# Gate and up projections with half of the depth as Strassen block products, weight sums made by accumulating transfers, and the feed-forward in two parts

## The chip, the cores and the metric

The kernel runs on one core of a Trainium2 chip. Its engines work in parallel, each through its own queue of instructions in order: TensorE (PE) multiplies, with its weight loads (PEld) beside it; VectorE (DVE) and ScalarE (ACT) work elementwise; GpSimd (POOL) does small work and issues transfers; SyncE (SP) issues transfers. The metric is the device time of one execution in microseconds (us), the median of several runs.

## The reference

One layer of a streaming encoder: 256 tokens, 2048 channels, float32. Three mixers with gates, an attention over a memory of 256 tokens, and a feed-forward. The change concerns the last of these alone:

```
def _swiglu(h, w_gu, w_down):
    g, u = jnp.split(h @ w_gu, 2, axis=-1)
    return (jax.nn.silu(g) * u) @ w_down

x = x + _swiglu(_rms(x, norm_ffn[i]), w_gu[i], w_down[i])
```

h is [256, 2048], w_gu [2048, 11264] (gate and up, 5632 columns each), w_down [5632, 2048].

## The kernel before

All large products keep float32 accuracy with the tensor engine's float32r kind: each operand is the sum of a high part, rounded to float32r, and a low part, and a product is three matmuls (high x high, high x low, low x high). The activations are split once into tiles such as `x2T_h` and `x2T_l`, [128 channels, 16 k-tiles, 256 tokens]. The weights are split as they come.

`gemm_i` is the product that carries most of the work: two tiles of 128 tokens by 512 columns of weights, accumulated over `nk` k-tiles of 128 channels in two banks of PSUM (`acc`). The weights come by `load_w` in blocks of four k-tiles, 1 MB each, into `raw` (two buffers), issued on SyncE. `split_w` makes `whi` (a cast on ScalarE, L116) and `wlo` (the difference on VectorE, L117) out of two k-tiles at a time, with four buffers each. Twelve matmuls use such a pair (L146 to L148: two token tiles, two k-tiles, three matmuls). A buffer of `whi` is free when these are done. At the end `evac` reads the two banks.

The stage of gate and up is a loop over 11 chunks of 512 columns. For each chunk there is one `gemm_i` for gate (evacuated by ScalarE with SiLU into `gt`, L1006), one for up (evacuated by VectorE, multiplied into `gt`, L1010), and `to_operand`, in which TensorE transposes the chunk (L812) and ScalarE and VectorE split it into `hT_h` and `hT_l` (L206, L207), which hold all 44 k-tiles. So the stage has 22 products. Then four `gemm_i` over 44 k-tiles multiply by w_down, and VectorE adds `x1`, the residual, into the output. `x2T_h` and `x2T_l` are made by `to_operand` after each quarter of the product with w_xo (L844: `x1` out of PSUM).

The order on each queue is fixed when the program is built, by a scheduler that follows the order of the code and two priorities: `WPRI` for the loads and splits of weights, `EPRI` for evacuations. A queue's instruction waits for semaphores of other queues or of transfers, and everything behind it waits with it.

## Time and profile before

| what | value |
|---|---|
| median of 3 runs | 2051.26 us (2050.34 to 2051.73) |
| the profiled execution, span from first to last instruction | 2048.7 us |
| stage of gate and up in it | 1294.40 to 1796.97 us, 22 products |
| w_down in it | 1796.97 to about 2044 us |
| HBM read, mean over the span | 374.06 MB, 184 GB/s with the writes |
| granted TensorE clock | 1.000 |

The span leaves out what lies before the first and after the last instruction. "Busy" is the time in which an engine has at least one instruction under way. A row of a group gives the line, the engine, the operation, the tile written and the tiles read, the shape, the count after an x, then busy time in us, the mean of one in ns, and the idle time of the engine ahead of them with what ended it. Rows of matmuls overlap, so their mean is not their cost. A row of transfers gives the tile, the queue, the count, the size and the median us from issue to landing. A row with two times joined by a colon is a stretch of the span: its length, then the busy time of PE, PEld, DVE, ACT and POOL with the number of instructions, the granted clock, the share of the transfer engines and GB/s. A row that begins with a time alone is one of the timeline: start, duration, engine, instruction.

### The profile page before, as it was taken

What the parts mean: (1) busy time and instruction counts of PE and PEld (TensorE: products, weight loads), DVE (VectorE), ACT (ScalarE), POOL (GpSimd) and SP (SyncE); (2) the same over time, 40 slices, a digit from 0 to 9 for tenths busy, and PEclk for the clock granted to TensorE, in tenths of its full rate; (3) what the DMA queues carried; (4) which work ended last, traced back from release to release, by engine and by line L of the source; (5) the groups of instructions that cost most, each with busy time, mean ns of one, the idle gap of its engine ahead of it and who ended that gap; (6) DMA issues with size and microseconds to landing.
All of it is one profiled execution on the core that took longest, in us unless ns stands there. A gap on an engine that the chain in (4) does not pass through costs nothing.

```text
span 2048.7 us, 25114 instructions
## 1 busy us (share of the span) xinstructions
PE 2039.7 (100%) x9880; PEld 1670.9 (82%) x9880; DVE 1251.7 (61%) x1804; ACT 966.0 (47%) x1308; POOL 73.7 (4%) x142
## 2 busy tenths in 40 slices
PE   9999999999999999999999999999999999999999
PEld 7998888777777788888888888888888888888887
DVE  7967885769887857645544655445444444444443
ACT  8555556544344445554544545444444444433332
POOL 1001202000000000011000100000000000000000
PEclk9999999999999999999999999999999999999999
DMA  8555455445555555765555444555555555555553
GB/s 309 186 174 165 152 179 186 155 172 174 180 183 188 192 171 195 271 218 175 175 185 185 144 145 164 185 185 185 185 185 185 185 185 185 185 185 195 195 197 132
DMA packets 60406, 377.78 MB, mean 184 GB/s; under 512 B 6912, under 2 KB 8064, under 8 KB 18816
## 3 DMA queue, kind: packets, MB, share of 16 engines
q1 hardware_dynamic: 56880, 367.42, 51.4%
q0 software_dynamic: 2112, 6.82, 1.2%
q10 hardware_dynamic: 1296, 1.95, 0.3%
q8 instruction: 77, 1.26, 0.2%
q14 instruction: 41, 0.34, 0.1%
HBM read 374.06 MB, written 2.10 MB: 184 GB/s over the span
## 4 chain that ended last, share of the span: by engine, by line
PE 99%; DVE 0%; DMA 0%; issue 0%; SPq 0%; ACT 0%; DVEq 0%; ACTq 0%
PE acc L146 29%; PE acc L148 29%; PE acc L147 28%; PE acc L169 2%; PE acc L170 2%; PE acc L171 2%; PE sm L422 1%; PE sm L812 1%; PE sm L952 1%; PE sm L978 1%; PE sm L449 1%; PE sm L215 0%; PE sm L896 0%; DMA raw<-in_w_in_dram 0%; DVE xT_l L210 0%
## 5 line engine op out<-in xcount | busy, mean ns | idle before, releaser
L117 DVE TENSOR_TENSOR wlo<-raw,whi 128x1024 fp32r<-128x1024 f32 (+2 forms) x700 | 834.7, 1194 | 697.7 <-ACT whi L116 694.3
L116 ACT CAST whi<-raw 128x1024 fp32r<-128x1024 f32 (+2 forms) x700 | 715.9, 1025 | 941.3 <-PE acc L148 816.9
L146 PE MATMUL acc<-whi,x2T_h 128*128 128x512 f32 x704 | 281.2, 399 | 0.0
L148 PE MATMUL acc<-whi,x2T_l 128*128 128x512 f32 x704 | 277.9, 395 | 0.0
L147 PE MATMUL acc<-wlo,x2T_h 128*128 128x512 f32 x704 | 277.2, 394 | 0.0
L147 PE MATMUL acc<-wlo,xT_h 128*128 128x512 f32 (+2 forms) x704 | 264.6, 377 | 1.8 <-DVE wlo L117 1.6
L148 PE MATMUL acc<-whi,xT_l 128*128 128x512 f32 (+2 forms) x704 | 265.3, 378 | 0.0
L146 PE MATMUL acc<-whi,xT_h 128*128 128x512 f32 (+2 forms) x704 | 262.4, 377 | 0.2
L148 PEld LDWEIGHTS acc<-whi,x2T_l 128*128 128x128 f32 x704 | 132.2, 188 | 33.4
L147 PEld LDWEIGHTS acc<-wlo,x2T_h 128*128 128x128 f32 x704 | 132.2, 188 | 31.4
L146 PEld LDWEIGHTS acc<-whi,x2T_h 128*128 128x128 f32 x704 | 132.2, 188 | 30.1
L147 PEld LDWEIGHTS acc<-wlo,xT_h 128*128 128x128 f32 x704 | 132.0, 188 | 29.8 <-DVE wlo L117 3.3
L146 PEld LDWEIGHTS acc<-whi,xT_h 128*128 128x128 f32 x704 | 131.5, 188 | 29.6 <-issue 3.2
L148 PEld LDWEIGHTS acc<-whi,xT_l 128*128 128x128 f32 x704 | 132.1, 188 | 27.8 <-issue 1.9
L146 PE MATMUL acc<-whi,hT_h 128*128 128x512 f32 x352 | 139.1, 395 | 0.0
L147 PE MATMUL acc<-wlo,hT_h 128*128 128x512 f32 x352 | 139.1, 395 | 0.0
L148 PE MATMUL acc<-whi,hT_l 128*128 128x512 f32 x352 | 139.0, 395 | 0.0
L148 PE MATMUL acc<-whi,eT_l 128*128 128x512 f32 x256 | 101.6, 397 | 0.0
L147 PE MATMUL acc<-wlo,eT_h 128*128 128x512 f32 x256 | 101.4, 396 | 0.0
L146 PE MATMUL acc<-whi,eT_h 128*128 128x512 f32 x256 | 101.2, 395 | 0.0
L169 PE MATMUL acc<-xT_h,whi 128*128 128x256 f32 x352 | 99.9, 284 | 0.0
L170 PE MATMUL acc<-xT_l,whi 128*128 128x256 f32 x352 | 99.5, 283 | 0.0
(375 smaller groups left out, 2837.0 us busy)
## 6 DMA issues: line engine op xcount, KB each, us to landing
raw<-in_w_gu_dram SPq DMA_DIRECT2D x88, 1024.0 KB, 4.8
raw<-in_w_in_dram SPq DMA_DIRECT2D x68, 1024.0 KB, 4.8
raw<-in_w_down_dram SPq DMA_DIRECT2D x44, 1024.0 KB, 4.7
raw<-in_w_xkv_dram SPq DMA_DIRECT2D x32, 1024.0 KB, 4.7
raw<-in_w_ii_dram SPq DMA_DIRECT2D x22, 1024.0 KB, 5.0
raw<-in_w_out_dram SPq DMA_DIRECT2D x16, 1024.0 KB, 5.0
raw<-in_w_xq_dram SPq DMA_DIRECT2D x16, 1024.0 KB, 4.8
raw<-in_w_xo_dram SPq DMA_DIRECT2D x16, 1024.0 KB, 4.8
```

The lines of the kernel that those rows point to most:

```text
L116: S.copy(hi[:, :n], raw[:, c0:c1])
L117: V.tensor_tensor(lo[:, :n], raw[:, c0:c1], hi[:, :n].bitcast(F32), ALU.subtract)
L146: PE.matmul(o, sh, h, start=(kt == 0), stop=False)
L147: PE.matmul(o, sh, lw, start=False, stop=False)
L148: PE.matmul(o, xl[:, kt, t * P:(t + 1) * P], h, start=False, stop=(kt == nk - 1))
L169: PE.matmul(po, h, xh[:, kt, :], start=(kt == 0), stop=False)
L170: PE.matmul(po, h, xl[:, kt, :], start=False, stop=False)
L171: PE.matmul(po, lo[:, j * P:(j + 1) * P], xh[:, kt, :], start=False, stop=(kt == nk - 1))
L422: PE.matmul(pb[:, i * T:(i + 1) * T], bT[q:q + 32, i, c, :], u[q:q + 32, c, :], start=True, stop=True, tile_position=(q, 0))
L449: PE.matmul(py[q:q + 32, :], cT[:, i, 4 * c + j, :], xs[j][:, i * T:(i + 1) * T], start=(i == 0), stop=(i == 1), tile_position=(0, q))
L812: PE.transpose(px[:, j * T + t * P:j * T + (t + 1) * P], srcs[t][:, (kp + j) * P:(kp + j + 1) * P], ident)
L952: PE.matmul(pS[:, t * T:(t + 1) * T], qx[:, qi, d, t * P:(t + 1) * P], kx[:, ki, d], start=(d + i == 0), stop=(d == 3 and i == 2))
```

## The change

The stage's product becomes `gemm_s`. Its first eight k-tiles are as before. The other eight are four pairs of k-tiles, and for each pair and the two token tiles the operand is seen as two by two blocks of 128x128, the weights as two by two blocks of 128x256 (`b11`, `b12`, `b21`, `b22`, each over four pairs, 1024 columns in all). Seven block products instead of eight give the result (Strassen's scheme in Winograd's form): four of them with sums of blocks of weights. The sums are made in place, in SBUF, by transfers that add (`wsum`, on GpSimd's queue): b11 += b12, b12 += b22, b22 += b11, b21 += b22, in this order. The weights of these eight k-tiles come into `sraw`, 2 MB with one buffer. The seven products go where their results are wanted in PSUM, or into a bank `sm` of their own; VectorE adds and subtracts them there (L238). The sums of the operand's blocks are made once, into `x2S_h` and `x2S_l`, by `pairs_operand`.

The feed-forward runs in two parts: chunks 0 to 5 of gate and up, then w_down over their 24 k-tiles, added into `x1`; then chunks 6 to 10, and w_down over their 20 k-tiles.

In the core of the diff line numbers are left out; the changed file's comments were removed, so its lines are numbered otherwise (the cast and the difference of `split_w` are L122 and L123 there, those of `parts` L202 and L203).

```diff
-KF = FF // P
+FF_PARTS = ((0, 6), (6, 11))
...
+    def wsum(dst, src):
+        with tc.high_priority(offset=WPRI):
+            nc.gpsimd.dma_start(dst, src, accum_op=ALU.add)
...
+    NS = 8
+    A11, A12, A21, A22, S1, S3, S2, S4 = range(8)
+    def gemm_s(xh, xl, sop, nk, src, off, evac, seven=True):
+        pp = [acc(), acc()]
+        n, no = 512, nk - NS
+        for k in range(0, no, 4):
...
+        raw = spool[0].tile([P, NS * n], F32, tag="sraw", name=nm("sraw"))
+        for i in range(2):
+            load_w(src[off:off + P * 4 * n].rearrange("(p f) -> p f", p=P), 4 * n,
+                   raw[:, i * 4 * n:(i + 1) * 4 * n])
+            off += P * 4 * n
+        rv = raw.rearrange("p (i q h c) -> p q h i c", q=2, h=2, c=256)
+        b11, b12, b21, b22 = (rv[:, q, h] for q in range(2) for h in range(2))
+        def parts(b):
+            hi = wp.tile([P, 1024], F32R, tag="whi", name=nm("whi"), bufs=4)
+            lo = wp.tile([P, 1024], F32R, tag="wlo", name=nm("wlo"), bufs=4)
...
+                S.copy(hi, b)
+                V.tensor_tensor(lo, b, hi.bitcast(F32), ALU.subtract)
+            return hi, lo
+        def product(o, i, b, start, stop):
+            hi, lo = b
+            for p in range(4):
+                sh, sl = sop(0, p, i), sop(1, p, i)
+                PE.matmul(o, sh, hi[:, p], start=start and p == 0, stop=False)
+                PE.matmul(o, sh, lo[:, p], start=False, stop=False)
+                PE.matmul(o, sl, hi[:, p], start=False, stop=stop and p == 3)
+        def kept(o):
+            u = spool[0].tile([P, 256], F32, tag="u", name=nm("u"), bufs=4)
+            with tc.high_priority(offset=EPRI):
+                S.copy(u, o)
+            return u
...
+        w21, w22, w11 = parts(b21), parts(b22), None
...
+        product(c(0, 0), A12, w21, False, False)
+        product(c(0, 1), S4, w22, False, True)
+        u1 = kept(side(A11, parts(b11)))
+        v(c(0, 0), c(0, 0), u1, ALU.add)
+        wsum(b11, b12)
+        wsum(b12, b22)
+        wsum(b22, b11)
+        u5 = kept(side(S1, parts(b11)))
+        p6 = side(S2, parts(b22))
+        wsum(b21, b22)
+        v(u1, p6, u1, ALU.add)
+        v(c(0, 1), c(0, 1), u5, ALU.add)
+        v(c(0, 1), c(0, 1), u1, ALU.subtract)
+        evac(0, pp[0])
+        product(c(1, 0), A22, parts(b21), False, True)
+        p7 = side(S3, parts(b12))
+        v(c(1, 1), c(1, 1), u5, ALU.add)
+        v(u1, p7, u1, ALU.add)
+        v(c(1, 0), c(1, 0), u1, ALU.add)
+        v(c(1, 1), c(1, 1), u1, ALU.subtract)
+        evac(1, pp[1])
+        return off
...
-        to_operand([x1[:, t, n * 512:(n + 1) * 512] for t in range(2)], gTh, gTl, 4 * n,
-                   "norm_ffn")
+        srcs = [x1[:, t, n * 512:(n + 1) * 512] for t in range(2)]
+        if n < 2:
+            to_operand(srcs, gT[0], gT[1], 4 * n, "norm_ffn")
+        else:
+            pairs_operand(srcs, n - 2, "norm_ffn")
...
-    for n in range(FF // 512):
...
-        off = gemm_i(gTh, gTl, KD, a["w_gu"], off, 512, evg)
-        off = gemm_i(gTh, gTl, KD, a["w_gu"], off, 512, evu)
-        to_operand(sg, hTh, hTl, 4 * n)
...
+    for c0, c1 in FF_PARTS:
+        nk = 4 * (c1 - c0)
+        hTh = p3.tile([P, nk, T], F32R, tag="hh", name=nm("hT_h"))
+        hTl = p3.tile([P, nk, T], F32R, tag="hl", name=nm("hT_l"))
+        for n in range(c0, c1):
...
+            gu_off = gemm_s(gT[0], gT[1], sop, KD, a["w_gu"], gu_off, evg)
+            gu_off = gemm_s(gT[0], gT[1], sop, KD, a["w_gu"], gu_off, evu)
+            to_operand(sg, hTh, hTl, 4 * (n - c0))
+        for n in range(4):
+            def ev(t, po, n=n, last=(c1 == FF // 512)):
...
+                    if not last:
+                        d = x1[:, t, n * 512:(n + 1) * 512]
+                        V.tensor_tensor(d, po, d, ALU.add)
+                        return
...
+            gemm_i(hTh, hTl, nk, a["w_down"], (n * FF + c0 * 512) * 512, 512, ev)
```

Three queues show where the change stands in the program. The names in the rows are the tiles with a running number; what stands in brackets are the queues whose semaphores the instruction waits for (DMASW are GpSimd's transfers, DMAHW SyncE's).

ScalarE before, in one product of the stage: the eight casts, each waiting for its load and for TensorE's use of the buffer.

```order
L116 CAST whi_12138<-raw_12136 128x1024 [waits DMAHW6_49,DVE_49,PE_49]
L116 CAST whi_12154<-raw_12136 128x1024 [waits DVE_49,PE_49]
L116 CAST whi_12172<-raw_12170 128x1024 [waits DMAHW7_49,DVE_49,PE_49]
L116 CAST whi_12188<-raw_12170 128x1024 [waits DVE_49,PE_49]
L116 CAST whi_12206<-raw_12204 128x1024 [waits DMAHW0_49,DVE_49,PE_49]
```

ScalarE after, from the first cast out of `sraw` to the first casts of the next product: the blocks 21, 22 and 11, then block 11 with its sum, two copies, blocks 22, 21 and 12 with their sums, and then the next product's n0 and n1.

```order
L202 CAST whi_12411<-sraw_12408 128x1024 [waits DMAHW4_49,DMAHW5_49,PE_49,Activation_49]
L202 CAST whi_12415<-sraw_12408 128x1024 [waits PE_49,Activation_49]
L202 CAST whi_12443<-sraw_12408 128x1024 [waits PE_49,Activation_49]
L202 CAST whi_12466<-sraw_12408 128x1024 [waits DMASW0_49,PE_49,Activation_49]
L217 COPY u_12460<-sm_12447 128x256 [waits PE_49]
L217 COPY u_12483<-sm_12470 128x256 [waits PE_49]
L202 CAST whi_12485<-sraw_12408 128x1024 [waits DMASW2_49,DVE_49]
L202 CAST whi_12507<-sraw_12408 128x1024 [waits DMASW3_49,DVE_49]
L202 CAST whi_12523<-sraw_12408 128x1024 [waits DMASW1_49,DVE_49]
L122 CAST whi_12565<-raw_12563 128x1024 [waits DMAHW6_49,DVE_49]
L122 CAST whi_12581<-raw_12563 128x1024 [waits DVE_49,PE_49]
```

Behind the plain casts now stand four that wait for GpSimd's transfers, and the next product's casts stand behind these.

GpSimd after, the transfers of one product (before it had none in this stage, its last rows being the reciprocal roots of the norm) and the first of the next:

```order
L115 DMA sraw_12201<-sraw_12201 128x4x256 [waits DMAHW0_49,DMAHW1_49,DMASW3_49,DVE_49]
L115 DMA sraw_12201<-sraw_12201 128x4x256 [waits DMASW4_49]
L115 DMA sraw_12201<-sraw_12201 128x4x256 [waits DMASW5_49]
L115 DMA sraw_12201<-sraw_12201 128x4x256 [waits DMASW6_49]
L115 DMA sraw_12408<-sraw_12408 128x4x256 [waits DMAHW4_49,DMAHW5_49,DMASW7_49,DVE_49]
```

The second, third and fourth wait for the transfer ahead of each.

TensorE after, at the end of one product and the start of the next: the last two block products (`acc_12132` from block 21, `sm_12320` from block 12) and the next product's first matmuls.

```order
L210 MATMUL acc_12132<-whi_12300,x2T_h 128x256 [waits Activation_49]
L210 MATMUL sm_12320<-whi_12316,x2T_h 128x256 [waits PE_49,Activation_49]
L211 MATMUL acc_12132<-wlo_12301,x2T_h 128x256 [waits DVE_49]
...
L185 MATMUL acc_12338<-whi_12342,x2T_h 128x512 [waits Activation_49]
L185 MATMUL acc_12339<-whi_12342,x2T_h 128x512
L211 MATMUL sm_12320<-wlo_12317,x2T_h 128x256 [waits DVE_49]
```

Two matmuls of the next product were moved ahead of the rest of the last block product, but none ahead of the product with block 21.

SyncE after: the load of `sraw` for the next product, between the loads of `raw` for that product and for the one after it.

```order
L101 DMA raw_12770<-in_w_gu_dram 128x2048 [waits DMAHW6_49,DVE_49]
L101 DMA raw_12804<-in_w_gu_dram 128x2048 [waits DMAHW7_49,DVE_49]
L101 DMA sraw_12838<-in_w_gu_dram 128x2048 [waits DMASW7_49,DMASW6_49,DMAHW0_49,DMASW5_49,DMAHW1_49,DMASW4_49,DVE_49]
L101 DMA sraw_12838<-in_w_gu_dram 128x2048
L101 DMA raw_12993<-in_w_gu_dram 128x2048 [waits DMAHW2_49,DVE_49]
```

The reload waits for all four of GpSimd's transfers of the product before, and for VectorE's last read; before, a load waited for a buffer of `raw` alone.

More of the change, by code (lines that the diff above doesn't have):

```diff
@@ L154, in gemm_i, with c, side, v @@
             evac(t, pp[t])
+        return off
[5 more added lines that the diff above has]
+        for k in range(0, no, 4):
+            raw = load_w(src[off:off + P * 4 * n].rearrange("(p f) -> p f", p=P), 4 * n)
+            off += P * 4 * n
+            for k2 in range(0, 4, 2):
+                hi, lo = split_w(raw, k2 * n, (k2 + 2) * n)
+                for t in range(2):
+                    for j in range(2):
+                        kt = k + k2 + j
+                        h, lw = hi[:, j * n:(j + 1) * n], lo[:, j * n:(j + 1) * n]
+                        sh = xh[:, kt, t * P:(t + 1) * P]
+                        PE.matmul(pp[t], sh, h, start=(kt == 0), stop=False)
+                        PE.matmul(pp[t], sh, lw, start=False, stop=False)
+                        PE.matmul(pp[t], xl[:, kt, t * P:(t + 1) * P], h, start=False, stop=False)
+        raw = spool[0].tile([P, NS * n], F32, tag="sraw", name=nm("sraw"))
+        for i in range(2):
+            load_w(src[off:off + P * 4 * n].rearrange("(p f) -> p f", p=P), 4 * n,
+                   raw[:, i * 4 * n:(i + 1) * 4 * n])
+            off += P * 4 * n
+        rv = raw.rearrange("p (i q h c) -> p q h i c", q=2, h=2, c=256)
[3 more added lines that the diff above has]
+            lo = wp.tile([P, 1024], F32R, tag="wlo", name=nm("wlo"), bufs=4)
+            hi, lo = (x.rearrange("p (i c) -> p i c", c=256) for x in (hi, lo))
+            with tc.high_priority(offset=WPRI):
+                S.copy(hi, b)
[13 more added lines that the diff above has]
+            return u
+        def c(t, h):
+            return pp[t][:, h * 256:(h + 1) * 256]
+        w21, w22, w11 = parts(b21), parts(b22), None
+        if not seven:
+            w11, w12 = parts(b11), parts(b12)
+            for t in range(2):
+                for h, q, w in ((0, 0, w11), (1, 0, w12), (0, 1, w21), (1, 1, w22)):
+                    product(c(t, h), 2 * t + q, w, False, q == 1 and h == 1)
+            for t in range(2):
+                evac(t, pp[t])
+            return off
+        def side(i, w):
+            o = sm()[:, :256]
+            product(o, i, w, True, True)
+            return o
+        def v(dst, x, y, op):
+            with tc.high_priority(offset=EPRI):
+                V.tensor_tensor(dst, x, y, op)
+        product(c(0, 0), A12, w21, False, False)
[19 more added lines that the diff above has]
+        evac(1, pp[1])
@@ L989, in tile_block @@
                      resid_evac(n, 2, lambda t: x1[:, t, n * 512:(n + 1) * 512]))
[L990 to L991 removed]
+        srcs = [x1[:, t, n * 512:(n + 1) * 512] for t in range(2)]
+        if n < 2:
+            to_operand(srcs, gT[0], gT[1], 4 * n, "norm_ffn")
+        else:
+            pairs_operand(srcs, n - 2, "norm_ffn")
     finish_rstd(2, 6)
[L993 removed]
     poolA.release()
     p3 = tc.alloc_tile_pool(name="p3", bufs=1)
[L998 removed]
@@ L999, in tile_block @@
-    hTl = p3.tile([P, KF, T], F32R, name="hT_l")
-    off = 0
-    for n in range(FF // 512):
-        sg = [t2k("gt", 2), t2k("gt", 2)]
-        def evg(t, po, sg=sg):
-            with tc.high_priority(offset=EPRI):
-                S.activation(sg[t], po, AF.Silu, scale=rst[:, 6 + t:7 + t])
-        def evu(t, po, sg=sg):
-            with tc.high_priority(offset=EPRI):
-                V.scalar_tensor_tensor(sg[t], po, rst[:, 6 + t:7 + t], sg[t], ALU.mult, ALU.mult)
-        off = gemm_i(gTh, gTl, KD, a["w_gu"], off, 512, evg)
-        off = gemm_i(gTh, gTl, KD, a["w_gu"], off, 512, evu)
-        to_operand(sg, hTh, hTl, 4 * n)
@@ L1014, in tile_block @@
-    off = 0
-    for n in range(4):
-        def ev(t, po, n=n):
-            o = t2k()
-            with tc.high_priority(offset=EPRI):
-                for c in range(0, 512, 256 if n == 3 else 512):
-                    d = slice(c, c + (256 if n == 3 else 512))
-                    g = slice(n * 512 + d.start, n * 512 + d.stop)
-                    V.tensor_tensor(o[:, d], po[:, d], x1[:, t, g], ALU.add)
-                    (nc.sync if c else nc.scalar).dma_start(out[t * P:(t + 1) * P, g], o[:, d])
-        off = gemm_i(hTh, hTl, KF, a["w_down"], off, 512, ev)
+    spool[0] = p3
```

51 lines of the change are left out of this document (47 added, 4 removed).

## The prediction

> **What bounds the kernel now.** I read the page first, its busy shares and its chain, then the stage of gate and up alone, then single rows for the prices.
>
> ```profile
> span 2048.7 us, 25114 instructions
> PE 2039.7 (100%) x9880; PEld 1670.9 (82%) x9880; DVE 1251.7 (61%) x1804; ACT 966.0 (47%) x1308; POOL 73.7 (4%) x142
> PE 99%; DVE 0%; DMA 0%; issue 0%; SPq 0%; ACT 0%; DVEq 0%; ACTq 0%
> 1294.40:1796.97 502.57, 502.57 (x2202) 405.31 (x2200) 244.67 (x225) 212.34 (x227) 1.47 (x4) 1.00 0.52 184
> L146 PE MATMUL acc<-whi,x2T_h 128*128 128x512 f32 x704 | 281.2, 399 | 0.0
> L117 DVE TENSOR_TENSOR wlo<-raw,whi 128x1024 fp32r<-128x1024 f32 x176 | 215.6, 1225 | 244.7 <-ACT whi L116 243.3
> L116 ACT CAST whi<-raw 128x1024 fp32r<-128x1024 f32 x176 | 184.6, 1049 | 266.1 <-PE acc L148 262.4 <-DMA raw<-in_w_gu_dram 3.7
> ```
>
> TensorE carries the chain: 99% of it, and in the stage of gate and up (fourth row: from the first product with x2T to the first with hT) it is busy for all 502.57 us, VectorE for half, ScalarE for less, the transfers for 0.52. One of the 22 products there costs 502.57 / 22 = 22.84 us. The splits stand idle waiting for TensorE (last row), so nothing but TensorE's own work sets the end. Work taken from TensorE is gain, as long as nothing that feeds it becomes later than it.
>
> The 394 to 399 ns of a row is not what a matmul costs: rows overlap. The spacing of the starts is.
>
> ```profile
> 2037.26 0.39 PE L146 MATMUL acc<-whi,hT_h 128*128 128x512 f32 x1
> ...
> 2044.02 0.39 PE L148 MATMUL acc<-whi,hT_l 128*128 128x512 f32 x1
> ```
>
> These are the first and the last of 30 rows in a run: 6.76 / 29 = 0.233 us for 512 columns. For 256 columns the first and the last of nine rows:
>
> ```profile
> 99.99 0.28 PE L169 MATMUL acc<-xT_h,whi 128*128 128x256 f32 x1
> ...
> 100.94 0.28 PE L171 MATMUL acc<-xT_h,wlo 128*128 128x256 f32 x1
> ```
>
> 0.95 / 8 = 0.119 us: half the columns, half the time, nothing lost to the smaller tile.
>
> **TensorE's own work.** Before, a product is 96 matmuls of 512 columns: 96 x 0.233 = 22.4 us. After, it is 48 of these (11.2 us) and seven block products of 12 matmuls with 256 columns (84 x 0.119 = 10.0 us): 21.2 us. The gain is 1.2 us a product, 22 x 1.2 = 27 us in all, if TensorE never waits.
>
> **What the four accumulating transfers put in its way.** They are one chain: the second reads what the first writes, the third the second's and so on, each waits for the landing of the one ahead. The first waits for VectorE to have split block 11, and that split needs a buffer of whi, of which there are four: it waits until TensorE is done with the third pair of k-tiles (n2 of n0 to n3). At its end, the fourth block (w21 with sums) is cast only when the last transfer has landed; on ScalarE the casts of the next product stand behind that one, and on SyncE the next 2 MB of sraw, since sraw has one buffer. TensorE's queue has nothing of the next product to do meanwhile. So per product there is a ring: landing of the fourth transfer (T) -> cast and split -> last two block products -> n0, n1, n2 of the next product -> split of block 11 -> four transfers -> T. Worked from T:
>
> ```profile
> L210 DVE SCALAR_TENSOR_TENSOR x2T_l<-sm,pp,x2T_h 128x256 fp32r<-128x256 f32 x4 | 1.7, 477 | 1.1 <-ACT x2T_h L209 1.1
> 1339.82 0.40 PE L148 MATMUL acc<-whi,x2T_l 128*128 128x512 f32 x1
> 1340.25 1.05 ACT L116 CAST whi<-raw 128x1024 fp32r<-128x1024 f32 x1 [1.75 <-PE acc L148]
> 1.48 4.31 PE L229 MATMUL acc<-ev 128*128 128x256 f32 x12 [1.48 <-DVE ev L226]
> 4.76 1.03 PE L229 MATMUL acc<-ev 128*128 128x256 f32 x4
> ```
>
> - Cast of w21 1.05, its low part 1.22: T + 2.3. Then a sum of 128x256 out of PSUM (0.48 by the first row, the nearest of that shape) and the low part of w12, 1.22: T + 4.0.
> - The product with w21, 12 matmuls of 256 columns. TensorE comes out of a wait here. At the kernel's start, after a wait, 12 equal rows (fourth row) begin at 1.48; the last four begin at 4.76 (fifth row). So the first eight take 3.28 / 8 = 0.41 us each, while the last four fit in 1.03: TensorE runs at about half its speed for some 3 us after it has stood, though the page's granted clock reads full there. I take double price: from T + 2.3, 11 more x 0.24 = T + 4.9.
> - The product with w12, 12 x 0.119 = 1.4: T + 6.3. n0, n1 and n2, 36 matmuls x 0.233 = 8.4: T + 14.7. Their casts and splits (three at 1.05 and 1.22) lie beside, ahead of TensorE.
> - A cast starts 0.43 us after the start of the last matmul that it waits for (second and third row), 0.2 after the end by spacing: 0.2 + 1.05 + 1.22 = 2.5. The first transfer can be issued at T + 17.2; some 0.3 for the hops between queues: T + 17.5.
>
> Beside it the reload of sraw: it may be issued when w12 is split, T + 4.0, and brings 2 MB.
>
> ```profile
> raw<-in_w_gu_dram SPq DMA_DIRECT2D x88, 1024.0 KB, 4.8
> GB/s 300 430 96 0 116 355 403 0 0 27 205 430 212 0 96 321 423 48 0 157 423 294 0 102 171 423 178 0 96 348 430 0 0 177 410 287 0 109 177 437
> ```
>
> One megabyte lands in 4.8 us, a second one behind it at the peak rate of the second row (430 GB/s, 1.2 us a column) 2.4 us later: T + 11.2; the three blocks out of it are cast and split by 1.05 + 3 x 1.22: T + 15.9. That is inside 17.5, by 1.6 us; between both loads in 4.8 and one after the other in 9.6 us it is T + 13.5 to T + 18.3, so it may cost up to 0.8 us a product. I take 17.5.
>
> So a product takes 17.5 + 4L, L being one accumulating transfer from issue to landing. L is in no row of this trace: nothing accumulates, nothing goes from SBUF to SBUF. The nearest rows are GpSimd's own loads and SyncE's by size:
>
> ```profile
> L868 POOL DMA_DIRECT2D gt<-in_x_dram x8: 536/536/538, 667.8 to 877.2; - x8
> DMA to landing us min/median/max: 3.3/4.1/5.0
> ...
> L661 POOL DMA_DIRECT2D t2k<-in_bias_dram x8: 536/566/626, 233.1 to 408.7; - x8
> DMA to landing us min/median/max: 2.7/4.8/5.7
> raw<-in_w_qk_dram SPq DMA_DIRECT2D x4, 512.0 KB, 3.2
> gt<-in_x_dram POOLq DMA_DIRECT2D x8, 256.0 KB, 4.1
> t2k<-in_bias_dram POOLq DMA_DIRECT2D x8, 192.0 KB, 4.8
> out_dram<-t2k ACTq DMA_DIRECT2D x2, 128.0 KB, 1.9
> ```
>
> GpSimd's 256 KB take 3.3 at best, 4.1 in the middle. SyncE's 512 KB take 3.2 and its 1024 KB 4.8, so 512 KB more cost 1.6. An accumulation of 512 KB reads 512 KB and what is there, another 512 KB: 768 KB more than the 256 KB row, 1.5 x 1.6 = 2.4. In the ring no load is under way while the four run, so I start from the best case: 3.3 + 2.4 = 5.7 us. Counted by bytes written alone it would be 3.3 + 0.8 = 4.1, and the whole 2051 + 22 x (17.5 + 16.4 - 22.84) = 2295; I count what is read, because the sum cannot be formed without both operands. The low end is 2.7, GpSimd's fastest landing of any size. The high end: the pieces are runs of 1 KB (512 of them against 128), so issuing may grow from 0.54 to 2.1 us, and on the slowest 256 KB row that is 5.0 + 2.4 + 1.6 = 9.0. The ends of the sum are then 28.3 and 53.5 us a product.
>
> The Trainium skill (Collectives: The Full Stack, the part on why ReduceScatter is half of AllGather) says that an adding transfer runs at half the rate because it emits two reads for each piece, not because the adding costs. By that rule L is the 5.7 above, by the rate of a plain copy 4.1, and the time 2435 or 2295. No row of this trace shows which.
>
> **The sum.** 17.5 + 4 x 5.7 = 40.3 us a product against 22.84: 17.5 us more, x 22 = 385 us. The gain of 27 us is in it, since TensorE's work is no longer the path.
>
> Edits that cost nothing. The feed-forward in two parts: eight additions of 128x512 into x1 (the second row below has this shape, 0.69 us) beside w_down's products; the second part's first write of hT waits for the end of the first part's w_down, but comes only two products later, over 42 us. The end of part one is a second change from up to w_down, but its first products read k-tiles finished long before. The operand's sums for the block products (16 additions of 128x128 with their splits) are wanted only after n3 of the first product, 11.2 us after TensorE begins there; if they come late it is once, a few us.
>
> ```profile
> L1010 DVE SCALAR_TENSOR_TENSOR gt<-acc,rst,gt 128x512 f32<-128x512 f32 x21 | 14.8, 744 | 0.0
> L207 DVE TENSOR_TENSOR hT_l<-sm,hT_h 128x512 fp32r<-128x512 f32 x20 | 12.9, 686 | 12.0 <-ACT hT_h L206 12.0
> ```
>
> VectorE's load per product is 11 splits x 1.22 + 7 sums x 0.48 + half of two evacuations at 0.74 + half of two low parts of hT at 0.69: 13.4 + 3.4 + 0.7 + 0.7 = 18.2 us, below 40.3 and also below 21.2. Of the seven sums only the one counted is in the ring.
>
> The sum is made on the profiled execution, 2048.7 us of span; the median of the runs is 2051.26, so 2.6 us lie outside it and stay. 2051.3 + 385 = 2436, taken as **2435 us**.
>
> **The rivals.**
>
> *Short transfers.* L may be near a small fixed price. At 2.7 to 3.3 us the sum gives 5.5 to 7.9 us more a product, 120 to 173 us: 2171 to 2224 us. For it: hardware-issued 512 KB land in 3.2. Against: GpSimd's never did below 3.3 at half the bytes. The Trainium skill (DMA: Bandwidth & Descriptors, Anatomy of one DMA) gives a GpSimd transfer 2.0 us + bytes / 436 GB/s, 3.2 us for 512 KB as a copy; by that estimate the time is 2215. The trace's 256 KB rows, 2.6 by the formula and 3.3 to 5.0 here, do not agree. Chance 10%, with everything below 2240.
>
> *Long transfers.* If GpSimd's descriptors for 1 KB pieces or the addition itself are slow, L is above 8 and the time above 2051 + 22 x (49.5 - 22.84) = 2637, up to 2725 at L = 9. For it: GpSimd's 192 KB in 1.5 KB rows already take 4.8 in the middle, longer than its 256 KB. Against: those ran beside weight loads. Chance 8%.
>
> *Hidden transfers, the other side.* If the four land ahead of TensorE's need, the path is TensorE's work again, and the time is 2051 - 27 = 2024. The place is the block product with w21: it must not wait. That needs 17.5 + 4L at most 22.84 to be even, L of 1.3 us; for the full gain about 1 us. For it: they are issued ahead, GpSimd has nothing else to do in this stage (4 rows, 1.47 us). Against: the fastest of all groups of transfers in the trace, 128 KB to the output, has a median of 1.9 us. Chance 2%; another 1% for landing within 0.2% of before.
>
> *Weights instead of sums.* The reload of sraw at its upper end (9.6 us) adds 0.8 x 22 = 18 us: 2453. It is inside the range.
>
> **How the numbers follow.** About 79% for the exposed chain at L of 3.5 to 8, 10% shorter, 8% longer, 3% not slower at all. The likeliest is the first, at 5.7: 2435. The range is its two ends, 17.5 + 14 = 31.5 us a product, 2051 + 190 = 2241, and 2637: 2240 to 2640; the ends of L beyond it hold the 18% left out. Within 0.2% (4 us, about what a measurement of this kernel can tell from no change) is 1%, faster 2%, slower 97%.
>
> **What would show it.** In the changed kernel's profile: TensorE no longer at 100% but at 21.6 / 40.3, near 55%, in the stage of gate and up, full elsewhere; a row of 88 transfers sraw<-sraw of 512 KB with a median near 5.7 us (this alone decides between the cases); ScalarE's casts of sraw waiting for these, with the third and fourth the longest; the stage some 887 us long. Matmuls with 256 columns at spacings of 0.119 where TensorE runs, 0.24 just after a wait. It would be wrong if TensorE's queue held work of the next product in those waits, or if the four transfers overlapped one another.

## The result, and the profile after

The changed kernel takes 2454.3 us (median of 4 runs, 2453.6 to 2454.7) against 2051.5 us before (2050.3 to 2052.9): 1.196 times the time, 95% interval 1.195 to 1.198. The prediction was 2435 us, 2240 to 2640. The profiled execution's span is 2452.7 us.

The page of the changed kernel, the rows that answer to those shown of before: the span, the busy shares, the granted clock in 40 slices, and the chain that ended last.

```profile
span 2452.7 us, 27437 instructions
PE 2140.2 (87%) x10672; PEld 1782.1 (73%) x10672; DVE 1397.5 (57%) x2066; ACT 1046.9 (43%) x1422; POOL 184.9 (8%) x230
PEclk9999999999999999999998777777799887777799
PE 73%; DMA 20%; issue 3%; ACT 2%; DVE 2%; POOL 0%; SPq 0%; ACTq 0%; DVEq 0%; POOLq 0%
```

TensorE carried 99% of the chain before; now it is 73%, and transfers that were nowhere on it hold 20%. TensorE's busy time has even grown (2039.7 to 2140.2 us) though it has less to do: the third row shows the clock at 0.7 to 0.8 in the slices of gate and up, full in w_down (the 9s between them and at the end).

The same stage, as two stretches (12 products of part one, 10 of part two: from the first product with x2T to the first with hT; columns as before):

```profile
1295.12:1787.80 492.68, 326.31 (x1623) 278.75 (x1622) 206.47 (x256) 160.42 (x188) 62.52 (x52) 0.76 0.60 153
1925.03:2335.50 410.47, 272.93 (x1350) 233.50 (x1349) 169.16 (x205) 129.05 (x148) 50.81 (x40) 0.75 0.59 147
```

Together 903.15 us where 502.57 us stood: 41.05 us a product instead of 22.84. That is 400.6 of the 402.8 us lost; w_down, the operand's sums and the second part cost next to nothing. TensorE is busy in 66% of it, at a granted clock of 0.75.

What waits, from the view of waits (engine and line, what it waited for, us in all, times, the longest), and then the view of the tile `sraw` on GpSimd, the transfers that are waited for (ns of an issue, first and last start, and us from issue to landing):

```profile
ACT whi L202 <- DMA sraw<-sraw: 379.9, 66, 7.5
POOL sraw L115 <- DMA sraw<-sraw: 296.5, 66, 5.1
PE sm L210 <- ACT whi L202: 226.9, 66, 9.0
```

```profile
L115 POOL DMA_DIRECT2D sraw<-sraw x88: 1255/1272/1389, 1308.7 to 2323.2; - x88
DMA to landing us min/median/max: 5.4/5.4/6.0
```

88 adding transfers, 5.4 us each, with hardly any spread. The first row is 66 waits, three a product: ScalarE's casts of the first, third and fourth sum (by the time block 12 is cast, its sum has landed). The second is GpSimd waiting for the transfer ahead of each, and the third TensorE behind ScalarE.

One whole turn of the ring, from GpSimd's rows of the timeline (start, duration of the issue, what GpSimd waited for) and the same turn in the chain that ended last (start, us, what):

```profile
1514.43 1.27 POOL L115 DMA_DIRECT2D sraw<-sraw  x1 [22.26 <-DVE wlo L203]
1520.14 1.26 POOL L115 DMA_DIRECT2D sraw<-sraw  x1 [4.44 <-DMA sraw<-sraw]
1525.83 1.27 POOL L115 DMA_DIRECT2D sraw<-sraw  x1 [4.42 <-DMA sraw<-sraw]
1532.06 1.26 POOL L115 DMA_DIRECT2D sraw<-sraw  x1 [4.96 <-DMA sraw<-sraw]
1555.64 1.27 POOL L115 DMA_DIRECT2D sraw<-sraw  x1 [22.31 <-DVE wlo L203]
```

```profile
1532.06 5.43 DMA sraw<-sraw
...
1537.57 1.05 ACT whi L202
1538.62 0.02 issue
1538.64 0.93 DVE wlo L203
...
1552.77 0.25 PE acc L187
1553.02 0.02 issue
1553.04 1.06 ACT whi L202
1554.10 0.02 issue
1554.12 1.24 DVE wlo L203
1555.36 0.28 issue
1555.64 5.43 DMA sraw<-sraw
```

The first transfers of two products in succession start at 1514.43 and 1555.64: 41.21 us. Four transfers end to end take 23.1 us of it (the fourth has landed at 1537.5), and 18.1 us go from there through cast, split, TensorE's last two block products, n0 to n2 of the next product, and block 11's cast and split, to the next first transfer. Each of these steps waits for the one ahead of it.

### The profile page after: what moved, and what is told of

It is laid out like the page before. It is cut to its first block, busy times and chain, and to the rows that moved or that the text cites. A ratio compares the mean times of both kernels' runs of the same rounds, so it can differ in the third digit from the quotient of the medians.

```text
span 2452.7 us, 27437 instructions
## 1 busy us (share of the span) xinstructions
PE 2140.2 (87%) x10672; PEld 1782.1 (73%) x10672; DVE 1397.5 (57%) x2066; ACT 1046.9 (43%) x1422; POOL 184.9 (8%) x230
## 4 chain that ended last, share of the span: by engine, by line
PE 73%; DMA 20%; issue 3%; ACT 2%; DVE 2%; POOL 0%; SPq 0%; ACTq 0%; DVEq 0%; POOLq 0%
DMA sraw<-sraw 19%; PE acc L152 17%; PE acc L154 17%; PE acc L153 17%; PE acc L185 3%; PE acc L187 2%; PE acc L186 2%; PE acc L274 2%; PE acc L275 2%; PE acc L276 2%; ACT whi L202 2%; DVE wlo L203 1%; PE sm L527 1%; PE sm L210 1%; PE acc L211 1%
## 5 line engine op out<-in xcount | busy, mean ns | idle before, releaser
L123 DVE TENSOR_TENSOR wlo<-raw,whi 128x1024 fp32r<-128x1024 f32 (+2 forms) x612 | 724.9, 1189 | 448.4 <-ACT whi L122 446.8
L122 ACT CAST whi<-raw 128x1024 fp32r<-128x1024 f32 (+2 forms) x612 | 621.2, 1021 | 719.7 <-PE acc L154 526.3
L203 DVE TENSOR_TENSOR wlo<-sraw,whi 128x1024 fp32r<-128x1024 f32 x154 | 188.1, 1224 | 457.9 <-ACT whi L202 457.6
L202 ACT CAST whi<-sraw 128x1024 fp32r<-128x1024 f32 x154 | 158.4, 1045 | 454.2 <-DMA sraw<-sraw 379.9
L210 PE MATMUL sm<-whi,x2T_h 128*128 128x256 f32 x176 | 70.6, 401 | 226.9 <-ACT whi L202 226.9
L210 PEld LDWEIGHTS sm<-whi,x2T_h 128*128 128x128 f32 x176 | 43.6, 248 | 244.1 <-ACT whi L202 244.1
L115 POOL DMA_DIRECT2D sraw<-sraw x88 | 111.9, 1271 | 913.2 <-DVE wlo L203 607.5
L186 PE MATMUL acc<-wlo,x2T_h 128*128 128x512 f32 x352 | 139.9, 397 | 0.0
L187 PE MATMUL acc<-whi,x2T_l 128*128 128x512 f32 x352 | 139.4, 396 | 0.0
L185 PE MATMUL acc<-whi,x2T_h 128*128 128x512 f32 x352 | 137.3, 422 | 0.0
```

What stands on the lines that cost most here:

```text
L115: nc.gpsimd.dma_start(dst, src, accum_op=ALU.add)
L122: S.copy(hi[:, :n], raw[:, c0:c1])
L123: V.tensor_tensor(lo[:, :n], raw[:, c0:c1], hi[:, :n].bitcast(F32), ALU.subtract)
L185: PE.matmul(pp[t], sh, h, start=(kt == 0), stop=False)
L186: PE.matmul(pp[t], sh, lw, start=False, stop=False)
L187: PE.matmul(pp[t], xl[:, kt, t * P:(t + 1) * P], h, start=False, stop=False)
```

## The experiments

Theory after the result: the time of a product is the larger of TensorE's own work (21.6 us) and a ring of 18.1 us + 4 x (one sum with its hop). Rivals: that Strassen's products themselves, or the two parts, cost time; that TensorE's clock after its waits is the larger loss; that the transfers are limited by the transfer engines and not by their order. Unless said otherwise, the diffs are against the changed kernel, and a ratio is against the kernel before with its 95% interval.

**1. No sums.** The four sums are left out; the seven products use the blocks as they come.

```diff
 def wsum(dst, src):
+    return
```

> This kernel leaves out the four sums of weight blocks of each product; everything else of the changed kernel stays, so its products use the plain blocks. Theory of the ring (18.1 us plus four serial transfers of 5.8 us a product): without the transfers nothing of the ring is left on the path, TensorE is full again, and a product costs its matmuls, 21.2 us and 0.4 of transposes: 2051 - 27 = 2024 us, up to 2045 if the reload of the single sraw buffer still shows. Rival, the added work: if the smaller matmuls, the sums on VectorE or TensorE's clock carry a good part of the 403 us, it stays above 2200.

Measured: 2029.8 us, ratio 0.990 (0.987 to 0.993), granted clock 1.0 throughout. So the sums carry the whole loss, and against the runs of before in the same round 20.9 us of the 27 us of TensorE's work come out as time: 21.9 us a product.

**2. The two parts alone.** The changed kernel with `gemm_i` in place of `gemm_s` and all of x2 made by `to_operand`.

```diff
-            gu_off = gemm_s(gT[0], gT[1], sop, KD, a["w_gu"], gu_off, evg)
+            gu_off = gemm_i(gT[0], gT[1], KD, a["w_gu"], gu_off, 512, evg)
```

> Only the feed-forward in two parts, with the product of the kernel before and no block products. Both theories: no change, 2051 plus or minus 4 us, since TensorE does the same matmuls and the eight added sums into x1 lie beside w_down's. If the seam between the parts costs, it shows here, some 5 to 10 us.

Measured: 2051.2 us, ratio 0.9998 (0.9988 to 1.0007). The parts cost nothing.

**3. The same transfers without the chain.** All four add a tile that never changes, so none needs the one ahead of it.

```diff
-            nc.gpsimd.dma_start(dst, src, accum_op=ALU.add)
+            nc.gpsimd.dma_start(dst, gT[0][:, 0:4].bitcast(F32), accum_op=ALU.add)
```

> The four accumulating transfers of a product stay, with the same 512 KB and the same 1 KB pieces, but their source is a tile that is not changed, so none waits for another (the sums are other sums). Ring theory: only the landing for block 11 is left on the ring, 18.1 + 5.5 = 23.6 us a product: 2051 + 22 x 0.8 = 2068, up to 2110 if four at a time land later than 5.4 us each. Rival, load: if the volume of the added transfers (88 x 512 KB) is what costs, they take as long together as one after the other, 23 us, and it stays above 2300.

Measured: 2237.5 us, ratio 1.091 (1.088 to 1.094). A miss for the theory by 130 us. The transfers do overlap, but each then takes nearly twice as long. The first and the fourth issue of a product and ScalarE's first cast of a sum, from the timeline, and then the landing of all 88, from the tile's view:

```profile
1523.32 1.28 POOL L115 DMA_DIRECT2D sraw<-x2T_h  x1 [22.99 <-DVE acc L238]
...
1530.24 1.26 POOL L115 DMA_DIRECT2D sraw<-x2T_h  x1 [1.53 <-DVE wlo L203]
...
1541.13 3.89 ACT L202 CAST whi<-sraw 128x1024 fp32r<-128x1024 f32 x4 [6.05 <-DMA sraw<-x2T_h]
```

```profile
DMA to landing us min/median/max: 5.7/9.9/11.7
```

17.8 us from the first issue to the first cast, against 23.1 in the chain. Of these, 6.9 us lie between the first and the fourth issue, since the second to fourth issues each wait for a split of VectorE (`wlo`), and 10.8 us are the landing of the fourth, which the cast waits for. Why a landing is so long stands in the view of the transfers, GB/s in 40 slices of 0.4 us (1514 to 1538 us) of the changed kernel, and in 40 slices of 0.625 us (1520 to 1545 us) of this one:

```profile
GB/s 0 0 0 20 172 177 169 176 155 3 0 0 0 102 177 174 172 176 72 0 0 0 20 176 174 174 174 154 2 0 0 0 0 126 176 176 172 176 48 0
```

```profile
GB/s 433 446 419 420 419 419 419 315 328 315 341 202 200 283 226 190 195 202 197 195 192 184 190 182 190 185 184 182 172 113 54 39 20 0 0 0 0 0 0 0
```

One adding transfer moves its 512 KB at some 175 GB/s, where weights come at 420. Overlapped, four of them share some 190 GB/s: at 175 the 2.1 MB need 12 us of the transfer engines however they are ordered. So "the chain is the loss" was only a part of it, and the rate is a second bound. A third part is the order: here all four block products with sums come behind that last landing, not two, and the first 28 of their 48 matmuls run at the low clock, nearly all 0.21 us apart. From the fourth landing to the next product's fourth issue it takes 22.2 us (1541.0 to 1563.2), where the changed kernel takes 18.1 from its last landing to the next first issue.

**4. Copies in place of additions**, and **5. half of the bytes**. Both keep the chain; the first adds nothing, the second adds two of the four pairs only.

```diff
-            nc.gpsimd.dma_start(dst, src, accum_op=ALU.add)
+            nc.gpsimd.dma_start(dst, src)                                     # 4
+            nc.gpsimd.dma_start(dst[:, 0:2], src[:, 0:2], accum_op=ALU.add)   # 5
```

> The four transfers stay as a chain, but copy instead of adding (the products then use copies of blocks). If the second read that adding needs is what makes a landing 5.4 us, a copy lands in about 4.1 (the price by bytes written in the prediction), and the time falls by 22 x 4 x 1.3 = 114 us to 2340. If the landing is set by issuing 512 pieces of 1 KB (1.27 us on GpSimd) and by the end of a transfer, it stays at 5.4 and the time at 2454.

> Each accumulating transfer moves two of the four pairs, 256 KB in 256 pieces (the sums of the other two pairs are left out). Landing by bytes read as in the prediction: 5.4 - 1.2 = 4.2 us, by bytes written 5.0. If the fixed part rules it stays near 5.4. The ring then gives 2454 - 22 x 4 x 1.2 = 2348, or 2419, or 2454. GpSimd's issue time of 1.27 us should fall towards 0.7.

Measured: copies 2248.9 us, ratio 1.097 (1.093 to 1.100); half of the bytes 2304.1 us, ratio 1.124 (1.120 to 1.127). The tile's rows, of the copies and of the halves (ns of an issue, then us to landing), and the view of the transfers of the copies, GB/s in 40 slices of 0.4 us:

```profile
L115 POOL DMA_DIRECT2D sraw<-sraw x88: 748/748/836, 1309.3 to 2121.8; - x88
DMA to landing us min/median/max: 3.3/3.3/5.3
```

```profile
L115 POOL DMA_DIRECT2D sraw<-sraw x88: 1176/1192/1299, 1309.2 to 2175.7; - x88
DMA to landing us min/median/max: 3.7/3.8/4.3
```

```profile
GB/s 0 0 0 0 328 369 338 277 0 0 0 0 0 317 328 369 297 0 0 0 0 0 317 358 348 287 0 0 0 0 0 358 338 358 256 0 0 0 0 0
```

A copy of 512 KB lands in 3.3 us at some 340 GB/s, an addition of the same blocks in 5.4 at 175: the addition runs at half the rate. (The copies also went in 576 pieces for four, the additions in 2112, so a part of the difference may be the size of the pieces; that was not separated.) Both landings are shorter than was expected (4.1 and 4.2 us). 256 KB less of adding saves 1.6 us; continued as a straight line, an estimate, 5.4 - 2 x 1.6 = 2.2 us would be left at no bytes. The issue on GpSimd hardly depends on the bytes (1.27 and 1.19 us) but on adding (0.75 without).

**6. A warm clock.** 84 matmuls a product on blocks that are there, into a bank that nobody reads, fill TensorE's waits.

```diff
-        u5 = kept(side(S1, parts(b11)))
-        p6 = side(S2, parts(b22))
+        def busy(w, m):
+            o = sm()[:, :256]
+            for i in range(m):
+                PE.matmul(o, sop(0, i % 4, A11), w[0][:, i % 4], start=True, stop=True)
+        w = parts(b11)
+        u5 = kept(side(S1, w))
+        busy(w, 60)
+        w = parts(b22)
+        p6 = side(S2, w)
+        busy(w, 24)
```

> As the changed kernel, with 84 idle matmuls of 256 columns a product put into TensorE's two long waits (60 after the product with S1, 24 after that with S2), writing to a bank that nobody reads. Nothing on the ring waits for them. If TensorE's half speed after a wait is on the path as the prediction has it (11 matmuls at 0.21 to 0.24 instead of 0.12 us), the step from the last landing to the next first transfer falls by 1.2 us, the time by 22 x 1.2 = 26 us to 2428. Rival: the split on VectorE or the reload of sraw sets that stretch, and the time stays at 2454 within 5 us.

Measured: 2439.9 us, ratio 1.189 (1.187 to 1.191), granted clock 0.982 instead of 0.909. The gain is 14.5 us of the 403, 0.66 us a product, but that is less than the clock cost. The fourth issue of a product and the first of the next, in one turn:

```profile
1531.04 1.26 POOL L115 DMA_DIRECT2D sraw<-sraw  x1 [5.94 <-DMA sraw<-sraw]
1553.07 1.27 POOL L115 DMA_DIRECT2D sraw<-sraw  x1 [20.76 <-DVE wlo L203]
```

22.0 us, where the changed kernel's turn above has 23.6. Over all turns but the one at the seam of the parts this step takes 22.7 us in the mean, 23.8 in the changed kernel: 1.1 us less. From the first to the fourth issue it takes 17.7 instead of 17.3, so 0.4 us of it are lost again. In five products the chain that ended last now also runs through the reload of `sraw`, which in the changed kernel it does at the first product alone. So by an estimate from this step the low clock cost the changed kernel at least 1.1 us a product, 24 us of the 403. The low clock that the page shows all through the stage is a consequence of the waits (0.982 with the waits filled), and most of it lies in time that would be waited anyway.

**7. The sums on GpSimd itself**, in the same order and with the same buffers.

```diff
-            nc.gpsimd.dma_start(dst, src, accum_op=ALU.add)
+            G.tensor_tensor(dst, dst, src, ALU.add)
```

> The four sums are made by GpSimd itself (tensor_tensor add on 128x1024) instead of by transfers; order and buffers as in the changed kernel. The ring stays, with four sums on GpSimd in place of four landings. VectorE does this shape in 1.22 us; GpSimd is expected at that or up to 3 us: 18.1 + 4 x 1.3 to 18.1 + 4 x 3 = 23.3 to 30.1 us a product, 2061 to 2211 us. The Trainium skill (GPSIMD Engine Reference, the table that compares it with VectorE) has 4.5 us for 2048 elements; by half of that the time is 2150. Rival: if the ring is not what costs, it stays above 2300.

Measured: 2192.6 us, ratio 1.069 (1.067 to 1.071). An addition takes 2.39 us (2.34 to 3.25), and a product 29.3 us, where the ring gives 18.1 + 4 x 2.45 = 27.9. The four together take 10.6 us, as some of them take up to 3.25.

**8. Sums made ahead.** Block 11 comes first, its product opens the product; two buffers of `sraw`; sums 1 and 2 stand ahead of the first four plain k-tiles, sums 3 and 4 between these and the other four; three parts, to make room. The sums are adding transfers as before.

```diff
-FF_PARTS = ((0, 6), (6, 11))
+FF_PARTS = ((0, 4), (4, 8), (8, 11))
...
-        raw = spool[0].tile([P, NS * n], F32, tag="sraw", name=nm("sraw"))
+        raw = spool[0].tile([P, NS * n], F32, tag="sraw", name=nm("sraw"), bufs=2)
...
+        u1 = kept(side(A11, parts(b11)))
+        wsum(b11, b12)
+        wsum(b12, b22)
+        plain(0)
+        product(c(0, 1), S4, parts(b22), False, False)
+        wsum(b22, b11)
+        product(c(0, 0), A12, parts(b21), False, False)
+        wsum(b21, b22)
+        plain(4)
```

> Transfers as in the changed kernel, but ahead of need: the product with block 11 comes first, blocks 22 and 21 between n0, n1 and n2, n3, two buffers of sraw, and the feed-forward in three parts (4, 4 and 3 chunks) to make room. TensorE then no longer waits inside a ring, but the chain of four is still one after the other on GpSimd: 4 x 5.78 = 23.1 us a product, longer than TensorE's 21.6. Ring theory: 22 x (23.1 - 22.84) = 6 us over before, 2057, up to 2110 where the landings meet the loads of weights. Rival, load: above 2200.

Measured: 2353.9 us, ratio 1.147 (1.145 to 1.149). A miss by some 250 us: the ring is only shortened, to 36.6 us a product. ScalarE in the timeline, between two products, and GpSimd's next issue:

```profile
1512.46 1.04 ACT L190 CAST whi<-sraw 128x1024 fp32r<-128x1024 f32 x1 [6.72 <-DMA sraw<-sraw]
...
1518.95 2.94 ACT L190 CAST whi<-sraw 128x1024 fp32r<-128x1024 f32 x3 [5.45 <-DMA sraw<-sraw]
...
1524.81 1.27 POOL L115 DMA_DIRECT2D sraw<-sraw  x1 [10.06 <-DVE wlo L191]
```

The casts of the next product's plain blocks stand on ScalarE's queue behind the casts that wait for the third and fourth landing. The next product's first sums wait for these casts and their splits (10.06 us). A second buffer does not open the ring where the order of one queue still closes it.

**9. The same with the sums on GpSimd:** run 8 with the line of run 7.

> As the kernel with the transfers ahead (block 11 first, two buffers of sraw, three parts), but the four sums are made by GpSimd itself. A chain of four at 1.3 to 3 us is 5 to 12 us, inside TensorE's 21.6 us a product, so TensorE should not wait: 2051 - 27 = 2024 us, up to 2035 with the seams of three parts and waits of a few tenths of a us. If sums on GpSimd and splits on VectorE disturb each other in SBUF, VectorE's 18.2 us a product grow beyond 21.6 and the time comes to 2050 or more.

Measured: 2113.1 us, ratio 1.030 (1.028 to 1.031). It missed the 2024 and came out on the side that was named for the case that the two engines disturb each other. ScalarE hardly waits for a sum any more (0.8 us in all), but VectorE has become slow. The page's VectorE shares of run 8 and of this one, and two rows of this one's timeline:

```profile
PE 2119.4 (90%) x10672; PEld 1773.7 (75%) x10672; DVE 1404.8 (60%) x2074; ACT 1043.2 (44%) x1422; POOL 184.0 (8%) x230
```

```profile
PE 2041.9 (97%) x10672; PEld 1698.8 (80%) x10672; DVE 1546.2 (73%) x2074; ACT 1046.7 (50%) x1422; POOL 310.0 (15%) x230
```

```profile
1406.91 5.74 POOL L115 TENSOR_TENSOR sraw<-sraw 128x1024 f32<-128x1024 f32 x2 [10.63 <-DVE wlo L191]
...
1407.41 2.98 DVE L123 TENSOR_TENSOR wlo<-raw,whi 128x1024 fp32r<-128x1024 f32 x1
```

The same 2074 instructions of VectorE take 141.4 us more: 1.61 us for each of the 88 additions on GpSimd. A split that meets one takes 2.98 us instead of 1.22. The Trainium skill (SBUF — State Buffer, on the two separate sides) says that VectorE and GpSimd share one pair of ports, and that an instruction of VectorE with two inputs in SBUF and one of GpSimd that reads SBUF shut each other out for their whole length; these rows agree.

**10 and 11. Sums on VectorE, in the order of run 8.** The diff is against run 8. In run 10 sums 1 and 3 are VectorE's and sums 2 and 4 stay transfers; in run 11 all four are VectorE's.

```diff
+    def vsum(dst, src):
+        with tc.high_priority(offset=WPRI):
+            V.tensor_tensor(dst, dst, src, ALU.add)
...
-        wsum(b11, b12)
+        vsum(b11, b12)
```

> As the run with block 11 first, two buffers of sraw and three parts, but sums 1 and 3 (b11 += b12, b22 += b11) are made by VectorE and sums 2 and 4 stay adding transfers; GpSimd adds nothing. Theory (GpSimd's additions slow VectorE's splits, and a chain of four transfers holds ScalarE's queue; with two transfers, each behind a block product of 8 matmuls or more, neither is there): VectorE has 11 splits and 2 sums at 1.22, 7 sums out of PSUM at 0.42 and some 0.7 of evacuations, 19.5 us a product, below TensorE's 21.6: no wait, 2051 - 27 = 2024, with a remainder of waits 2024 to 2035. Rival (two landings of 5.5 us still stand in ScalarE's or VectorE's queue ahead of the next product's splits): 2 x 5.5 exposed in part, 24 to 27 us a product, 2076 to 2140. Rival (VectorE's queue cannot be filled above some 85% because its instructions wait for PSUM and casts in turn): 23 us a product, near 2051.

> The same with all four sums on VectorE: no transfer adds and GpSimd adds nothing. Theory (work on VectorE at its unhindered prices decides): 15 instructions at 1.22, 7 at 0.42, 0.7 of evacuations, 22.0 us a product, just above TensorE's 21.6: 2051 - 22 x 0.8 = 2033, up to 2060 if VectorE's waits add 1.2 us a product; slower than the run with two transfers by 5 to 25 us if that has no exposed landing, faster than it if the landings are what waits. Rival (VectorE cannot be the bound at over 95%): 2070 to 2100.

Measured: run 10 2152.8 us, ratio 1.049 (1.047 to 1.050); run 11 2039.6 us (2038.9 to 2042.7), ratio 0.9945 (0.9932 to 0.9957). Run 10 lies above even the first rival's 2140, and by its mechanism: ScalarE and VectorE wait for the two transfers, and a landing takes 8.7 us in the middle, beside weight loads:

```profile
ACT whi L194 <- DMA sraw<-sraw: 103.8, 14, 9.1
DVE sraw L115 <- DMA sraw<-sraw: 70.3, 19, 6.7
```

```profile
DMA to landing us min/median/max: 5.4/8.7/10.8
```

Run 11 is faster than the kernel before by 0.55%: the only complete kernel of the study that is. Its stretch of eight products (from the second group of matmuls of the first to the first with hT), and from the timeline the row with which the first of them begins:

```profile
1304.70:1478.70 174.00, 173.56 (x1069) 154.86 (x1070) 165.87 (x192) 105.42 (x120) 0.00 (x0) 0.99 0.51 187
```

```profile
1303.76 0.58 PE L202 MATMUL sm<-whi,x2T_h 128*128 128x256 f32 x1 [6.86 <-ACT whi L194]
```

21.75 us a product: TensorE is full again, with VectorE busy in 95% of the time just behind it (20.7 us a product, less than the 22.0 that were added up, since its instructions overlap a little). The last row is a cost of the new order: the first product begins with block 11, whose load is late, and TensorE stands for 6.86 us. That would be 6.86 of the 9.8 us between this and the 2029.8 us of run 1; a first product in the old order was not tried.

**12. Sums on VectorE in the changed kernel's own order.**

```diff
-            nc.gpsimd.dma_start(dst, src, accum_op=ALU.add)
+            V.tensor_tensor(dst, dst, src, ALU.add)
```

> The changed kernel with one line other: the four sums are made by VectorE in place of the transfers; order, one buffer of sraw and two parts stay. It tells whether the new order of the run with all sums on VectorE (block 11 first, two buffers, three parts) was needed, or only cheap sums. Ring theory (time from the fourth sum to the first sum of the next product 18.1, and four sums of 1.22 with hops of 0.05 behind it): 18.1 + 4 x 1.27 = 23.2 us a product against 22.84, and some low-clock time as far as TensorE waits: 2059, 2050 to 2070. Rival (no ring is left once the sums have no hops, and VectorE's 22.0 us of work a product is what bounds, as in the other order): 2038 to 2045.

Measured: 2073.3 us, ratio 1.011 (1.009 to 1.013), 23.8 us a product. Just above the theory's upper end, and clearly not the rival's 2045. So the ring is still there with sums of 1.22 us, and what runs 8 to 11 changed together (block 11 first, a second buffer, three parts) made the difference; which of the three it was, no run tells. The first two sums of a product, its fourth, and the first two of the next, on VectorE:

```profile
1522.22 2.49 DVE L115 TENSOR_TENSOR sraw<-sraw 128x1024 f32<-128x1024 f32 x2
...
1527.25 1.22 DVE L115 TENSOR_TENSOR sraw<-sraw 128x1024 f32<-128x1024 f32 x1
...
1544.89 2.48 DVE L115 TENSOR_TENSOR sraw<-sraw 128x1024 f32<-128x1024 f32 x2
```

The four take 6.3 us here from start to end, 6.8 in the mean of the turns (without the seam), and not 4 x 1.27 = 5.1: other work of VectorE stands between them. From the end of the fourth to the next first it takes 16.4 us, 16.9 in the mean, and not 18.1; TensorE hardly waits here, and its clock is full (0.999). The two differences nearly cancel. The reload of the one buffer has a part as well: ScalarE waits for it 14 times, 42.7 us in all, and in five products after the first the chain that ended last runs through it.

```profile
ACT whi L202 <- DVE sraw L115: 47.5, 38, 3.0
ACT whi L202 <- DMA sraw<-in_w_gu_dram: 42.7, 14, 5.4
```

The runs with the changed kernel's order and buffers against the ring (a sum with its hop; 18.1 + four of them; measured: 22.84 + the median less 2051.5, by 22):

| run | one sum | ring, us a product | measured |
|---|---|---|---|
| changed kernel | 5.78 | 41.2 | 41.1 |
| 5, half of the bytes | 4.1 | 34.5 | 34.3 |
| 4, copies | 3.6 | 32.5 | 31.8 |
| 7, on GpSimd | 2.45 | 27.9 | 29.3 |
| 12, on VectorE | 1.27 | 23.2 | 23.8 |
| 1, none | 0 | 18.1, TensorE 21.6 | 21.9 |

One sum covers them, to 1.4 us. The 18.1 is taken from the changed kernel, so its row is no test; the others are, with two limits. The 18.1 holds some 1.1 us of low clock, which the kernels with short waits do not pay, and in run 12 that is made up for by other work between the sums. And run 3 does not follow it: with one landing of 9.9 it would give 28.0 us, and 31.3 were measured, for the order above.

## Why the prediction was right

- **The place and the form.** Right: the ring from the fourth landing back to the first transfer is on the chain in every link that was named, in that order. TensorE's queue did have nothing of the next product in the waits. Predicted 40.3 us a product, measured 41.1; a stage of 887 us, measured 903.
- **The price of a transfer, L.** 5.7 predicted, 5.4 measured. The step between two transfers is 5.71, 5.69 and 6.23 us in the turn shown, since 0.28 to 0.85 us pass between a landing and GpSimd's next issue; the sum had no term for that. The four together: 22.8 predicted, 23.1 measured in this turn and 22.7 in the mean of all. So two small errors cancelled, and that the sum came so close is in this part luck.
- **Why L is what it is.** The prediction counted both operands as read, and took 5.7 and not 4.1. The halves give 1.6 us for 256 KB of adding, 0.8 us for each of the 256 KB read from two places, as SyncE's row had it (1.6 for 512 KB). The copies give 3.3 us. The Trainium skill's rule that was weighed there (Collectives: The Full Stack, on why ReduceScatter is half of AllGather) agrees with these runs as far as they go: half the rate, 175 against 340 GB/s, with the size of the pieces not separated. The estimate for a copy by the Trainium skill (DMA: Bandwidth & Descriptors, Anatomy of one DMA), 3.2 us, agrees with the 3.3 measured. The rival "short transfers" took that figure for the addition, which takes 5.4.
- **From the landing to the next transfer.** 17.5 predicted, 18.1 measured in the turn shown, 18.3 in the mean of the turns without the seam: this step is where the sum was short. The cast and split, n0 to n2 and block 11 are nearly as priced. The matmuls of 256 columns after a wait start 0.21 us apart and not 0.24, from 1540.5 to 1542.6, and the product with block 21 ends 0.25 us later than counted. What had no term: the two matmuls of the next product that were moved ahead still run at the low clock (0.85 us for both, 0.4 more than counted), and two transposes of the chunk before take 0.2.
- **The clock.** Right: 11 x 0.12 = 1.3 us a product was counted, and with the clock kept up the step from the fourth transfer to the next first one fell by 1.1 in the mean. The 2428 us expected of run 6 missed by 12 us, of which the 0.4 us a product that the steps between the transfers grew make 9.
- **The reload** of `sraw` was said to be inside the ring, with up to 0.8 us of cost. Right: in the turn shown ScalarE's first cast after it starts 11.2 us after the fourth landing (1548.67), as counted for the landing. ScalarE waits 27.9 us for it in all, but the chain that ended last runs through it at the first product alone, so by this chain it is no part of the 0.8 us a product by which the sum was short.
- **The signs.** TensorE was to be busy near 55% of the stage and is in 66%: its matmuls at the low clock are busy for longer, 599 us in place of 22 x 21.6 = 475. ScalarE's longest waits were to be the third and the fourth; in the turn shown they are the first and the third (7.08, 6.39 and 5.23 us).
- **The edits costed at nothing** cost nothing: run 2, and the 400.6 of 402.8 us that lie in the stage.
- **Hidden transfers.** The even point was put at a sum of 1.3 us. Run 12 has sums of 1.22 and is 1.1% slower: right to within 0.3 us a sum, on the optimistic side. The full gain needed "about 1 us"; in that order no engine made a sum that fast.
- **What the prediction had too simple:** it said that it would be wrong "if the four transfers overlapped one another". Run 3 let them, and the kernel was still 9% slower. The rate of adding transfers and the order of the block products are further bounds behind the chain, and ScalarE's queue (run 8) another.

## What to carry to other kernels

Work that is taken from a full engine is gain only if the ring of waits that the new work closes stays shorter than what is left on that engine: write down, for one turn, every wait from a buffer's last use back to its next first use, and count the landings in it. A transfer that adds is a slow adder, 5.4 us for 512 KB where VectorE takes 1.22, and a chain of them, or casts that wait for them on an in-order queue, is paid in full; an idle transfer engine does not make it free. Here VectorE just had the room (20.7 us busy of 21.75 a product with the sums), and adding there gave 0.55%, with the first dependent block first and a second buffer.

## What the runs showed of the hardware

- Adding transfers within SBUF: 5.4 us for 512 KB, 3.8 for 256 KB, at some 175 GB/s while they move; four at a time share 190 GB/s. Beside weight loads the median was 8.7 us. A plain copy: 3.3 us at some 340 GB/s. GpSimd is held for 1.27 us by the issue of an addition, 0.75 by that of a copy.
- An addition of 128x1024 in float32 takes 1.22 us on VectorE and 2.39 us on GpSimd, but GpSimd's also lengthens VectorE's own work: by 1.61 us for each addition in run 9, where they stand among VectorE's splits, and by (1454.6 - 1397.5) / 88 = 0.65 us in run 7, by the busy times of its page and of the changed kernel's. In run 9's order that is more than the addition takes on VectorE itself.
- The prediction said that the granted clock reads full where TensorE, at the kernel's start, ran at half its speed (1.48 to 4.76 us). The clock's records in that profile begin only 4.45 us into the span, so that was no reading. In the changed kernel it does not read full after a wait. The stretches are the fourth transfer, the low-clock matmuls behind it, and n0 to n2:

```profile
1532.06:1537.50 5.44, 3.29 (x12) 2.71 (x12) 1.23 (x1) 0.28 (x1) 1.26 (x1) 0.50 0.66 96
1541.36:1544.74 3.38, 3.38 (x21) 3.19 (x20) 3.38 (x5) 1.14 (x2) 0.00 (x0) 0.69 0.67 221
1544.86:1552.77 7.91, 7.91 (x36) 6.37 (x36) 6.65 (x9) 3.15 (x3) 0.00 (x0) 1.00 1.01 428
```
